# One block of 512 tokens in the last third of an input projection

## The chip, the cores and the metric

The kernel runs on one core of a Trainium2 chip. The metric is the device time of one execution in microseconds (us). The engines are TensorE (PE in the profile, its weight loads PEld), VectorE (DVE), ScalarE (ACT), GpSimd (POOL) and SyncE (SP), whose queue issues nearly all transfers.

## What is computed

One layer of a streaming encoder on 2064 tokens (16 learned meta tokens and 2048 of the sequence), 1024 features, all in float32. The part that matters here is the input projection, one product whose 2824 output columns are shared among three groups of heads:

```python
p = rms_norm(h, norm_mix_pre[l]) @ w_in[l]          # (2064, 1024) @ (1024, 2824)
pa, pb, pc = ...                                    # RG-LRU, forgetting attention (q, k, v, gate), RWKV-7
oa = rg_lru_group(xa, ya, ...)                      # a scan over tokens
ob = forgetting_attention_group(q, k, v, f_logit, f_bias)
oc = rwkv7_group(pc, ...)                           # a recurrence over tokens
h = h + rms_norm(concat([oa, ob, oc]) @ w_out[l], norm_mix_post[l])
f = causal_dwconv(rms_norm(h, norm_ffn_pre[l]) @ ffn_up[l], ffn_conv[l])
h = h + rms_norm((gelu(gate) * val) @ ffn_down[l], norm_ffn_post[l])
return h[:, 16:]
```

## The kernel before

Precision comes from splitting: every operand is held as a high and a low part in a reduced float32 format, and a product is three matmuls, high by high, high by low, low by high (`mm3`, L150 to L152).

The input projection goes over the tokens in three parts. Tokens come in 17 tiles, the first of 16 meta tokens and sixteen of 128. `w_in_tokens` (L158) cuts them into two blocks for each part: 400 and 384 tokens, 384 and 384, 256 and 256. `w_in_norm` (L165) loads each tile, scales it (L104 to L108), transposes it on TensorE (L121) and writes the high part with ScalarE (L127) and the low part with VectorE (L128) into the block's tiles `xh` and `xl`, which are allocated anew for each part under the tags `xh0`, `xl0`, `xh1`, `xl1` in a pool with one buffer for each tag.

`w_in_part` (L258) then runs over the output columns. First come the eight forget-gate columns (`w_in_gate`, L248 and L249), then 24 units of 128 columns: eight for RWKV, four for the LRU, four each for keys, values and queries. For a unit the weights are loaded and split (L143 to L145), and `w_in_step` (L186) does 24 matmuls for each block into one bank of PSUM (`psp`), then evacuates: for RWKV, LRU and values with either ScalarE or VectorE in turn (L55, L57), for queries and keys as a high part by ScalarE (L200, tile `sth`, two buffers) and a low part by VectorE (L201, tile `stl`, one buffer), each stored to scratch memory in DRAM (L202, L203). Values are turned by TensorE one step later (L217). The last two units run block by block, so that a block's tokens are done with before the other's:

```python
for block in blocks:
    for w, kind, c0 in last:
        step(w, block, kind, c0)
    yield
```

Beside the projection run the recurrences: `recurrences` (L1866) first handles the forget gate of each block (`gate_block`, L341), then LRU and RWKV blocks. They are advanced by `Beside`: at every `yield` of the projection 1.5 steps of the recurrences are emitted (`PACE`, L1827); what is left is emitted when the projection is over. The order of the program is not the order on the engines: the tile framework plans each engine's queue ahead (`TileContext(nc, schedule_with_timeline_sim=True)`, L2115), so that in the trace recurrence matmuls stand in the middle of a projection unit. On the chip each queue runs in its planned order.

After the third part the projection's pools are closed and attention (`Attn`) takes their memory; its constant rows are set by GpSimd (L435, L436, tile `k`) and VectorE (L431 to L433, tile `q`), and its loads are issued by SP (L470 to L499). A tile laid over old memory waits until the old tiles there have been read. Attention's scores are L635 and L636, its row maxima L509 to L515. Then follow the output projection (`pswo`) and the feed-forward layer (`psu`, `psd`).

Of the kernel before, what the change touches and what calls it, by code (L numbers as in the profile page):

```python
# [8 lines left out]
F32 = mybir.dt.float32  # L9
F32R = mybir.dt.float32r  # L10
# [8 lines left out]
P = 128  # L19
D = 1024  # L20
KD = D // P
# [126 lines left out]
def mm3(nc, out, ah, al, bh, bl, first, last, more=False):  # L148

    nc.tensor.matmul(out, ah, bh, start=first, stop=False, skip_group_check=more)  # L150
    nc.tensor.matmul(out, ah, bl, start=False, stop=False, skip_group_check=more)  # L151
    nc.tensor.matmul(out, al, bh, start=False, stop=last, skip_group_check=more)  # L152
# [5 lines left out]
def w_in_tokens(part):  # L158

    tiles = [(0, META)] + [(META + P * i, P) for i in range(SEQ // P)]  # L160
    cuts = ((0, 4, 7), (7, 10, 13), (13, 15, 17))[part]
    return [tiles[a:e] for a, e in zip(cuts, cuts[1:])]


def w_in_norm(core, pools, psum, x, meta, gain, part):  # L165
    blocks = []
    for b, tl in enumerate(w_in_tokens(part)):
        t0 = tl[0][0]
        n = sum(r for _, r in tl)
        hi = pools["xn"].tile([P, KD, n], F32R, tag=f"xh{b}", name=core.n("xh"))  # L170
        lo = pools["xn"].tile([P, KD, n], F32R, tag=f"xl{b}", name=core.n("xl"))
        blocks.append((t0, n, tl, hi, lo))
    for t0, n, tl, hi, lo in blocks:
        for s, rows in tl:
            src = meta if s < META else x[s - META : s - META + rows, :]
            norm_transpose(core, pools, psum, src, rows, gain, [(hi, lo, s - t0, 0, rows)])
    return blocks
# [8 lines left out]
def w_in_step(core, pools, psum, weights, block, kind, c0, scr):  # L186

    nc = core.nc
    wh, wl = weights
    st = pools["st"]  # L190
    t0, n, tl, hi, lo = block
    ps = psum.tile([P, 512], F32, tag="mm", name=core.n("psp"))
    for k in range(KD):
        mm3(nc, ps[:, :n], wh[:, k], wl[:, k], hi[:, k], lo[:, k], k == 0, k == KD - 1)
    if kind in ("q", "k"):
        sc = 0.125 if kind == "q" else 1.0
        r0 = c0 - (512 if kind == "q" else 1024)
        oh = st.tile([P, 400], F32R, tag="sth", name=core.n("sth"))
        ol = st.tile([P, 400], F32R, tag="stl", name=core.n("stl"), bufs=1)
        nc.scalar.activation(oh[:, :n], ps[:, :n], AF.Copy, scale=sc)  # L200
        nc.vector.scalar_tensor_tensor(ol[:, :n], ps[:, :n], sc, oh[:, :n], op0=ALU.mult, op1=ALU.subtract)  # L201
        nc.sync.dma_start(scr[kind + "h"][r0 : r0 + P, t0 : t0 + n], oh[:, :n].bitcast(F32))  # L202
        nc.sync.dma_start(scr[kind + "l"][r0 : r0 + P, t0 : t0 + n], ol[:, :n].bitcast(F32))  # L203
        return
    o = st.tile([P, 400], F32, tag="sth", name=core.n("stp"))
    core.evac(o[:, :n], ps[:, :n])
    if kind != "v":
        r0 = c0 if kind == "a" else c0 - 2056 + A_ROWS
        nc.sync.dma_start(scr["p"][r0 : r0 + P, PAD + t0 : PAD + t0 + n], o[:, :n])
        return  # L210

    def turn():

        r0 = c0 - 1536
        pt = psum.tile([P, 4, P], F32, tag="mm", name=core.n("psv"))
        for i, (s, rows) in enumerate(tl):
            nc.tensor.transpose(pt[:rows, i], o[:, s - t0 : s - t0 + rows], core.ident[:])  # L217
        ot = st.tile([P, 4, P], F32, tag="stv", name=core.n("stv"), bufs=1)
        i0 = 0
        if tl[0][1] < P:  # L220
            s, rows = tl[0]
            core.evac(ot[:rows, 0], pt[:rows, 0])
            nc.sync.dma_start(scr["v"][s : s + rows, r0 : r0 + P], ot[:rows, 0])
            i0 = 1
        m = len(tl)
        core.evac(ot[:, i0:m], pt[:, i0:m])
        s = tl[i0][0]
        nc.sync.dma_start(
            scr["v"][s : s + P * (m - i0), r0 : r0 + P].rearrange("(j p) c -> p j c", p=P), ot[:, i0:m]
        )  # L230

    return turn


def w_in_gate(core, pools, psum, w_in, blocks, scr):

    nc = core.nc
    c0 = 2048
    raw = pools["w"].tile([P, KD, 8], F32, tag="fraw", name=core.n("fraw"), bufs=1)
    nc.sync.dma_start(raw[:], w_in[:, c0 : c0 + 8].rearrange("(k p) c -> p k c", p=P))  # L240
    w = pools["w"].tile([P, KD, P], F32R, tag="wh", name=core.n("fw"))
    nc.vector.memset(w[:].bitcast(F32), 0.0)
    nc.scalar.activation(w[:, :, 0:8], raw[:], AF.Copy)
    nc.vector.tensor_tensor(w[:, :, 32:40], raw[:], w[:, :, 0:8], op=ALU.subtract)
    for t0, n, tl, hi, lo in blocks:
        ps = psum.tile([P, 512], F32, tag="mm", name=core.n("psf"))
        for k in range(KD):
            nc.tensor.matmul(ps[:, :n], w[:, k], hi[:, k], start=k == 0, stop=False)  # L248
            nc.tensor.matmul(ps[:, :n], w[:, k], lo[:, k], start=False, stop=k == KD - 1)  # L249
        a = pools["st"].tile([8, 400], F32, tag="sth", name=core.n("fa"))  # L250
        nc.scalar.activation(a[:, :n], ps[32:40, :n], AF.Copy)
        o = pools["st"].tile([8, 400], F32, tag="stl", name=core.n("fo"), bufs=1)
        nc.vector.tensor_tensor(o[:, :n], ps[0:8, :n], a[:, :n], op=ALU.add)
        nc.sync.dma_start(scr["f"][:, t0 : t0 + n], o[:, :n])
    yield
# [85 lines left out]
def gate_block(core, R, f_bias, scr, tl):  # L341

    nc = core.nc
    t0, n = tl[0][0], sum(r for _, r in tl)
    if t0 == 0:
        core.fb = core.const.tile([NH, 1], F32, name="fb")
        nc.sync.dma_start(core.fb[:], f_bias.rearrange("(h o) -> h o", o=1))

    def new(s, dt=F32):
        return R.t([NH, 400], s, dt)[:, :n]  # L350

    x = new("k")
    nc.sync.dma_start(x, scr["f"][:, t0 : t0 + n])
    a = new("r")
    nc.scalar.activation(a, x, AF.Abs, bias=core.fb[:])
    nc.scalar.activation(a, a, AF.Exp, scale=-1.0)
    nc.scalar.activation(a, a, AF.Ln, bias=1.0)
    nc.vector.tensor_scalar(x, x, core.fb[:], 0.0, op0=ALU.add, op1=ALU.min)
    nc.vector.tensor_tensor(x, x, a, op=ALU.subtract)

    o = META if t0 else 0
    call = R.t([NH, 512], "sq")[:, : o + n]
    c = call[:, o:]
    if o:
        nc.vector.tensor_copy(call[:, :o], core.ctail[:])
    nc.vector.tensor_tensor_scan(
        c, core.ones_8[:].to_broadcast([NH, n]), x, core.ctail[:, META - 1 :], op0=ALU.mult, op1=ALU.add
    )
    nc.vector.tensor_copy(core.ctail[:], c[:, n - META :])
    ch, cl = new("k", F32R), new("r", F32R)  # L370
    nc.scalar.activation(ch, c, AF.Copy, scale=-1.0)
    nc.vector.scalar_tensor_tensor(cl, c, -1.0, ch, op0=ALU.mult, op1=ALU.subtract)
    nc.sync.dma_start(scr["ch"][:, t0 : t0 + n], ch.bitcast(F32))
    nc.sync.dma_start(scr["cl"][:, t0 : t0 + n], cl.bitcast(F32))
    j0, full = (t0 - o) // P, (o + n) // P
    ps = R.pe()
    for i in range(full):
        nc.tensor.transpose(ps[:, NH * i : NH * i + NH], call[:, P * i : P * i + P], core.ident[:NH, :NH])
    js = slice(j0, j0 + full)
    nc.vector.tensor_copy(core.ccol[:, js].rearrange("p j h -> p (j h)"), ps[:, : NH * full])  # L380
    if t0 + n == T:
        ps = R.pe()
        nc.tensor.transpose(ps[:META, :NH], call[:, P * full :], core.ident[:NH, :NH])
        nc.vector.tensor_copy(core.ccol[:META, NKT - 1], ps[:META, :NH])
        js = slice(j0, j0 + full + 1)
    ps = R.pe()
    w = (js.stop - js.start) * NH
    nc.tensor.matmul(
        ps[:, :w], core.ones_row[:], core.ccol[0:1, js].rearrange("p j h -> p (j h)"), start=True, stop=True
    )  # L390
    nc.vector.tensor_copy(core.cref[:, js].rearrange("p j h -> p (j h)"), ps[:, :w])
# [1474 lines left out]
def recurrences(core, R, lk, f_bias, scr, blocks, part):  # L1866


    for blk in blocks:
        gate_block(core, R, f_bias, scr, blk[2])  # L1870
        yield
    for b in ((0, 1, 2), (3, 4, 5), (6, 7, 8))[part]:
        yield from lru_block(core, R, scr, lk, b)
        gen = R.block(b)
        while next(gen) != R.SOLVED:
            yield
        yield from R.ending
        R.ending = gen
# [240 lines left out]
```

## Time and profile before

| what | value |
|---|---|
| time, three runs | 3123.35, 3115.73 and 3134.21 us, median 3123.35 |
| profiled execution | 3122.89 us, of which the span of instructions is 3121.2 us |
| granted TensorE clock, mean | 0.962 |
| busy: PE, DVE, ACT, POOL | 2925.9, 2251.1, 1452.4, 1301.9 us |

The input projection fills the stretch from 44.7 to 869.3 us: part one to 290, part two to about 627, part three from 635 to 869. Attention lies between there and about 1600 us, with the rest of the recurrences beside it until about 1200 us; the feed-forward layer takes the rest.

A row of a group gives line, engine, operation, tile written and tiles read, shapes and number, then busy time, mean ns of one, and the idle time of its engine ahead of it with what ended it. A row of the order of time gives start, duration, engine and line, and in brackets the idle time ahead of it and what ended it. SPq is SP's queue issuing a transfer. A row of a window gives its bounds and length, busy time and number of instructions of PE, PEld, DVE, ACT and POOL, the granted clock, and the share and rate of the transfers. Ends of matmuls are modelled, and consecutive matmuls overlap in the records.

### The profile page before, as it was taken

To read this page: it belongs to the slowest core of one execution; us is meant where nothing else is said; L and a number is where in the kernel's file an instruction comes from. 1 tells how busy PE (TensorE), PEld (TensorE's weight loads), DVE (VectorE), ACT (ScalarE), POOL (GpSimd) and SP (SyncE) were. 2 spreads that over 40 slices of the span, in tenths; PEclk is the share of its full clock that TensorE was granted. 3 is DMA by queue.
4 is the path that set the end of the run, shared out by engine and by line. 5 is a ranking of instruction groups with operands and counts; after the bars stand their busy time and mean duration, and the time that the engine had idled before them with its cause. 6 is when DMAs were issued, how large, how long until landed. Compare 5 with 4: busy or idle time off the path is not lost. (4 is left out here: it accounts for less than half of the span.)

```text
span 3121.2 us, 52484 instructions
## 1 busy us (share of the span) xinstructions
PE 2925.9 (94%) x18488; PEld 2492.2 (80%) x18488; DVE 2251.1 (72%) x4585; ACT 1452.4 (47%) x2716; POOL 1301.9 (42%) x1436
## 2 busy tenths in 40 slices
PE   6988999999978999999998899999999999999998
PEld 6987998999855664665576899899999999787776
DVE  6247655676688778877758898888778787547777
ACT  4135334344544444445533555566666665324332
POOL 3310001101134365446733568743533334547665
PEclk9999999999988788999999899999999999999999
DMA  6664333353353235544236555565665565535454
GB/s 205 226 204 137 101 97 100 107 140 104 97 143 81 64 84 142 130 117 107 65 107 201 162 171 158 167 193 170 166 166 166 166 188 162 174 105 167 143 161 142
DMA packets 456503, 443.72 MB, mean 142 GB/s; under 512 B 82496, under 2 KB 373514, under 8 KB 453408
## 3 DMA queue, kind: packets, MB, share of 16 engines
q1 hardware_dynamic: 455856, 439.99, 48.3%
q8 instruction: 145, 2.38, 0.3%
q14 instruction: 118, 0.97, 0.1%
q0 software_dynamic: 384, 0.39, 0.0%
HBM read 314.39 MB, written 125.87 MB: 141 GB/s over the span
## 5 line engine op out<-in xcount | busy, mean ns | idle before, releaser
L150 PE MATMUL psu<-xo,uw 128*128 128x344 f32 x1848 | 594.9, 326 | 25.2 <-DVE vb L1684 10.4
L151 PE MATMUL psu<-xo,uw 128*128 128x344 f32 x1848 | 597.1, 323 | 0.7 <-DVE xo L1529 0.7
L152 PE MATMUL psu<-xo,uw 128*128 128x344 f32 x1848 | 586.5, 322 | 0.0
L150 PE MATMUL psp<-xh,wh 128*128 128x384 f32 (+2 forms) x1152 | 382.0, 332 | 0.0
L152 PE MATMUL psp<-xh,wl 128*128 128x384 f32 (+2 forms) x1152 | 379.1, 330 | 3.0 <-DVE wl L145 3.0
L151 PE MATMUL psp<-xl,wh 128*128 128x384 f32 (+2 forms) x1152 | 378.2, 328 | 0.0
L150 PEld LDWEIGHTS psu<-xo,uw 128*128 128x128 f32 x1848 | 350.3, 190 | 31.4 <-DVE vb L1684 12.4
L1529 DVE TENSOR_TENSOR uw<-uq,uw 128x512 fp32r<-128x512 f32 x352 | 327.5, 935 | 59.5 <-ACT uw L1528 55.8
L151 PEld LDWEIGHTS psu<-xo,uw 128*128 128x128 f32 x1848 | 351.7, 190 | 1.1 <-DVE xo L1529 1.1
L152 PEld LDWEIGHTS psu<-xo,uw 128*128 128x128 f32 x1848 | 350.0, 190 | 0.0
L1528 ACT ACTIVATE uw<-uq 128x512 fp32r<-128x512 f32 x462 | 286.9, 627 | 102.8 <-PE psu L152 48.8
L640 ACT ACTIVATE p<-sc,bias 128x512 f32<-128x512 f32 (+4 forms) x352 | 197.6, 590 | 217.3 <-PE sc L636 181.8
L1640 DVE SCALAR_TENSOR_TENSOR uy<-psu,ffn_cols,uy 128x342 f32<-128x342 f32 (+1 forms) x396 | 224.0, 567 | 72.0 <-ACT uy L1638 70.9
L679 POOL TENSOR_TENSOR acc<-acc,p 128x512 f32<-128x512 f32 (+3 forms) x208 | 230.5, 1111 | 78.7 <-DVE acc L679 37.9
L1646 POOL TENSOR_TENSOR uy<-uy,uy 128x342 f32<-128x342 f32 (+1 forms) x132 | 146.3, 1109 | 224.5 <-DVE uy L1640 79.2
L152 PEld LDWEIGHTS psp<-xh,wl 128*128 128x128 f32 x1152 | 220.1, 191 | 10.3 <-issue 5.5
L150 PEld LDWEIGHTS psp<-xh,wh 128*128 128x128 f32 x1152 | 219.9, 191 | 7.1 <-issue 4.7
L151 PEld LDWEIGHTS psp<-xl,wh 128*128 128x128 f32 x1152 | 220.0, 191 | 6.4 <-issue 4.1
L1529 POOL TENSOR_TENSOR uw<-uq,uw 128x512 fp32r<-128x512 f32 x110 | 155.9, 1417 | 164.2 <-ACT uw L1528 137.8
L512 DVE TENSOR_REDUCE mc<-mx 128x1 f32<-128x400 f32 (+5 forms) x320 | 171.5, 554 | 55.3 <-PE mx L509 53.9
L1529 DVE TENSOR_TENSOR fo<-u,fo 128x896 fp32r<-128x896 f32 x88 | 104.4, 1187 | 118.6 <-ACT fo L1528 118.6
L1528 ACT ACTIVATE fo<-u 128x896 fp32r<-128x896 f32 x88 | 81.0, 922 | 230.9 <-POOL u L1756 120.9
(451 smaller groups left out, 6612.6 us busy)
## 6 DMA issues: line engine op xcount, KB each, us to landing
uq<-in_ffn_up_dram SPq DMA_DIRECT2D x220, 256.0 KB
uq<-scr_us SPq DMA_DIRECT2D x176, 256.0 KB
raw<-in_w_in_dram SPq DMA_DIRECT2D x72, 512.0 KB
scr_us<-uq SPq DMA_DIRECT2D x88, 256.0 KB
u<-scr_ff SPq DMA_DIRECT2D x88, 256.0 KB
scr_ff<-uy SPq DMA_DIRECT2D x110, 171.0 KB
q<-scr_qh SPq DMA_DIRECT2D x96, 128.0 KB
ds<-in_ffn_down_dram SPq DMA_DIRECT2D x10, 1024.0 KB
```

Of the source, the lines that this page charges most:

```text
L150: nc.tensor.matmul(out, ah, bh, start=first, stop=False, skip_group_check=more)
L151: nc.tensor.matmul(out, ah, bl, start=False, stop=False, skip_group_check=more)
L152: nc.tensor.matmul(out, al, bh, start=False, stop=last, skip_group_check=more)
L512: self.reduced = nc.vector.tensor_reduce(mc[:rows, i, ci : ci + 1], ps[:rows, :full], axis=AX.X, op=ALU.max)
L640: last = nc.scalar.activation(p[:rows, :w], ps[:rows, :w], AF.Exp, bias=bias[:rows, j : j + 1])
L679: eng.tensor_tensor(a, ps_[0][0][:rows, c0:n] if start and i == 1 else a, p[:rows, : n - c0], op=ALU.add)
L1528: core.nc.scalar.activation(hi, src, AF.Copy)
L1529: (eng or core.nc.vector).tensor_tensor(lo, src, hi, op=ALU.subtract)
L1640: stt(y[:, :n], src[:, i : n + i], cw[:, 44 * i + cc : 44 * i + cc + 1], y[:, :n], op0=ALU.mult, op1=ALU.add)
L1646: core.pooled = nc.gpsimd.tensor_tensor(v[:, :n], g[:, :n], v[:, :n], op=ALU.mult)
```

## The change

The third part is cut into one block of 512 tokens. The high and low parts of the tokens live in two tiles of 784 columns, allocated once for all parts; the first block of a part lies at column 0, the second at column 400. The block of 512 of the third part therefore lies across what the two blocks of 384 of the second part used. Staging tiles grow from 400 to 512 columns. The forget gate of the block of 512 is still handled in two halves. As the last two units yield once for each block, the third part yields 24 times, not 25.

```diff
 def w_in_tokens(part):
 
     tiles = [(0, META)] + [(META + P * i, P) for i in range(SEQ // P)]
-    cuts = ((0, 4, 7), (7, 10, 13), (13, 15, 17))[part]
+    cuts = ((0, 4, 7), (7, 10, 13), (13, 17))[part]
     return [tiles[a:e] for a, e in zip(cuts, cuts[1:])]
+
+CUT, COLS, BANK = 400, 784, 512
 
 def w_in_norm(core, pools, psum, x, meta, gain, part):
     blocks = []
+    if part == 0:
+        core.tokens = [pools["xn"].tile([P, KD, COLS], F32R, tag=s, name=core.n(s)) for s in ("xh", "xl")]
     for b, tl in enumerate(w_in_tokens(part)):
         t0 = tl[0][0]
         n = sum(r for _, r in tl)
-        hi = pools["xn"].tile([P, KD, n], F32R, tag=f"xh{b}", name=core.n("xh"))
-        lo = pools["xn"].tile([P, KD, n], F32R, tag=f"xl{b}", name=core.n("xl"))
+        hi, lo = (t[:, :, CUT * b : CUT * b + n] for t in core.tokens)
         blocks.append((t0, n, tl, hi, lo))
...
-        oh = st.tile([P, 400], F32R, tag="sth", name=core.n("sth"))
-        ol = st.tile([P, 400], F32R, tag="stl", name=core.n("stl"), bufs=1)
+        oh = st.tile([P, BANK], F32R, tag="sth", name=core.n("sth"))
+        ol = st.tile([P, BANK], F32R, tag="stl", name=core.n("stl"), bufs=1)
...
-    o = st.tile([P, 400], F32, tag="sth", name=core.n("stp"))
+    o = st.tile([P, BANK], F32, tag="sth", name=core.n("stp"))
...
 def recurrences(core, R, lk, f_bias, scr, blocks, part):
 
-    for blk in blocks:
-        gate_block(core, R, f_bias, scr, blk[2])
-        yield
+    for _, n, tl, *_ in blocks:
+        for tiles in (tl,) if n <= CUT else (tl[: len(tl) // 2], tl[len(tl) // 2 :]):
+            gate_block(core, R, f_bias, scr, tiles)
+            yield
```

More of the change, by code (lines that the diff above doesn't have):

```diff
@@ L249, in w_in_gate @@
             nc.tensor.matmul(ps[:, :n], w[:, k], lo[:, k], start=False, stop=k == KD - 1)
-        a = pools["st"].tile([8, 400], F32, tag="sth", name=core.n("fa"))
+        a = pools["st"].tile([8, BANK], F32, tag="sth", name=core.n("fa"))
         nc.scalar.activation(a[:, :n], ps[32:40, :n], AF.Copy)
-        o = pools["st"].tile([8, 400], F32, tag="stl", name=core.n("fo"), bufs=1)
+        o = pools["st"].tile([8, BANK], F32, tag="stl", name=core.n("fo"), bufs=1)
         nc.vector.tensor_tensor(o[:, :n], ps[0:8, :n], a[:, :n], op=ALU.add)
```

## The prediction

> **What bounds the kernel now.** I read the page first, then busy time by windows around the part of the kernel that the change touches, then single rows in order of time.
>
> ```profile
> PE 2925.9 (94%) x18488; PEld 2492.2 (80%) x18488; DVE 2251.1 (72%) x4585; ACT 1452.4 (47%) x2716; POOL 1301.9 (42%) x1436
> PEclk9999999999988788999999899999999999999999
> ```
>
> TensorE is busy for 94% of the span, and its granted clock is near full but for slice 23 and slices 12 to 16 (78 us each, so 858 to 1248 us). The change acts on the third part of the input projection; its own stretch is found by the first gate matmul of that part (635.4 us) and the end of its last projection matmul (869.3 us).
>
> ```profile
> core 0: us, PE busy (x) PEld busy (x) DVE busy (x) ACT busy (x) POOL busy (x), PEclk, DMA share, GB/s
> 635.40:869.30 233.90, 231.70 (x2430) 210.13 (x2428) 160.49 (x370) 110.45 (x202) 21.98 (x41) 0.99 0.40 110
> 869.30:920.00 50.70, 32.30 (x286) 21.80 (x287) 45.42 (x130) 19.16 (x39) 15.33 (x21) 0.76 0.74 171
> 920.00:980.00 60.00, 49.92 (x423) 31.39 (x423) 54.87 (x164) 29.45 (x63) 27.31 (x47) 0.90 0.33 83
> 980.00:1100.00 120.00, 108.02 (x1008) 75.74 (x1006) 89.08 (x275) 50.15 (x115) 56.05 (x94) 0.76 0.27 69
> 1100.00:1200.00 100.00, 92.39 (x640) 57.41 (x638) 82.39 (x247) 38.77 (x82) 49.43 (x75) 0.84 0.39 91
> ```
>
> In the 233.9 us of the third part TensorE is busy for 231.7: it alone sets the pace there, and what shortens its queue shortens the stretch. Right behind it the picture turns: between 869.3 and 920 TensorE works 32.3 of 50.7 us and VectorE 45.4, and until 980 VectorE works 54.9 of 60. So time won on TensorE before 869 is kept only if VectorE is not handed work into the next 110 us in exchange.
>
> **The matmuls.** The third part runs 24 weight columns over its 512 tokens. Today each column takes 8 x 3 matmuls for each of two blocks of 256; the change makes it 8 x 3 of 512 columns.
>
> ```profile
> L150 PE MATMUL psp<-xh,wh 128*128 128x256 f32 x384 | 112.7, 294 | 0.0
> L151 PE MATMUL psp<-xl,wh 128*128 128x256 f32 x384 | 110.8, 289 | 0.0
> L152 PE MATMUL psp<-xh,wl 128*128 128x256 f32 x384 | 111.6, 291 | 0.0
> ```
>
> That is 1152 matmuls now and 576 afterwards; the gate adds 32 now, 16 afterwards. Their mean of 290 ns cannot be used as a price, since matmuls overlap: the price is the distance from start to start in an undisturbed stretch. Here are the first and last rows of three such stretches: 14 starts of 256 columns, 20 of 384, and 12 of 512 columns (output projection, the same triple of lines).
>
> ```profile
> 700.01 0.28 PE L151 MATMUL psp<-xl,wh 128*128 128x256 f32 x1
> ...
> 701.55 0.28 PE L152 MATMUL psp<-xh,wl 128*128 128x256 f32 x1
> 583.01 0.34 PE L150 MATMUL psp<-xh,wh 128*128 128x384 f32 x1
> ...
> 586.35 0.34 PE L151 MATMUL psp<-xl,wh 128*128 128x384 f32 x1
> 1601.69 0.40 PE L152 MATMUL pswo<-woh,ml 128*128 128x512 f32 x1
> ...
> 1604.22 0.39 PE L151 MATMUL pswo<-wol,mh 128*128 128x512 f32 x1
> ```
>
> 256 columns: 1.54 / 13 = 0.1185 us. 384: 3.34 / 19 = 0.1758. 512: 2.53 / 11 = 0.2300. Two of 256 cost 0.2369, one of 512 costs 0.2300: 0.0069 saved for each pair, and 592 pairs make 4.1 us. The straight line through 256 and 384 would put 512 at 0.2331, that is 3.8 ns a pair and 2.2 us; this is the low end. A gain of twice 4.1 us, for a clock that steps down under dense work less often, is the far end. I take 4.1, since the 512 row is a measurement of the very form that is added. Weight loads are halved too, but they ran beside matmuls already (the distance grows with the columns, 57 ns for 128 of them, and almost nothing is left at zero columns), so nothing more comes from them.
>
> The Trainium skill (TensorE: Matmul & The Clock Gate, Back-to-back issue gap) gives a fixed cost of about 2.5 ns for each matmul above its columns at 2.4 GHz; by that the pairs would save 592 x 2.5 ns = 1.5 us. The rows differ (118.5 ns where it has 109), and the sum goes by the rows. The same section also gives a sustained figure of 131 ns for 512 columns; the 230 ns here speak against that, and no weight is given to it.
>
> **The start of the third part.** The gate matmuls of the first block start today as soon as two of the four token tiles are split. With one block they need all four.
>
> ```profile
> 635.41 0.37 PE L248 MATMUL psf<-xh,fw 128*128 128x256 f32 x1
> 637.63 1.09 PE L1189 MATMUL rps<-rwsc,rwxu 64*64 64x128 f32 x16
> 638.65 1.20 PE L1201 MATMUL rps<-rww,rwsc 128*64 128x64 f32 x32
> 637.56 1.87 DVE L128 TENSOR_TENSOR xl<-pst,xh 128x512 fp32r<-128x512 f32 x3
> 306.24 1.22 PE L981 MATMUL eps<-rwwa,wa_up 64*128 64x256 f32 x2 [11.31 <-ACT rwe L982]
> ```
>
> VectorE finishes the low halves of the last tiles at 639.4 (three operations of about 0.62 us from 637.56). The first four of eight row groups of all tiles are there after the second, at 638.8, so the gate starts 3.4 us later than 635.41. Cover is the recurrence: the L1189 and L1201 groups (1.09 and 1.20 us) that ran in the middle of the gate can run ahead of it if their own inputs are there, which leaves 1.1 us. Bounds: 0 with full cover, and 11.3 us, which is what the border between parts one and two shows when a recurrence matmul that waits for ScalarE stands ahead of ready projection work in TensorE's queue. I take 2 us, near the 1.1 to 3.4. Everything before (parts one and two) keeps its instructions; the two fixed buffers can be overwritten region by region, and the two borders already write new tokens only after the old part's last matmuls, so that edit costs nothing there.
>
> **Paced steps.** The last two weight columns yield once for each block, so the third part yields 24 times instead of 25, and at PACE 1.5 that moves 1.5 recurrence steps from beside the projection to behind it. In TensorE time a step costs (233.9 - 1184 x 0.1185) / 37.5 = 2.5 us, so 3.7 us leave the stretch.
>
> ```profile
> L145 DVE TENSOR_TENSOR wl<-raw,wh 128x1024 fp32r<-128x1024 f32 x24 | 29.1, 1213 | 2.4 <-ACT wh L144 2.2
> L57 DVE COPY stp<-psp 128x256 f32<-128x256 f32 x19 | 8.0, 421 | 4.2 <-PE psp L152 4.1
> L201 DVE SCALAR_TENSOR_TENSOR stl<-psp,sth 128x256 fp32r<-128x256 f32 x15 | 6.8, 452 | 12.1 <-DMA scr_kl<-stl 8.9 <-DMA scr_ql<-stl 2.7 <-ACT sth L200 0.5
> ```
>
> Their VectorE share is (160.5 - 29.1 - 8.0 - 6.8) / 37.5 = 3.1 us a step: 4.7 us arrive in a stretch where VectorE is the busy one. Bounds -3.7 and +4.7; I take 0, because what TensorE loses VectorE gets. The skipped weight-sum step is run at the end of the same loop and stays covered.
>
> **Evacuations and stores.** One operation of 512 columns (L128 above, 0.62 us) takes the place of two of 0.42 to 0.45: some 0.2 us less for each, on an engine with 73 us idle in the stretch, so nothing on the path. The L201 row shows more: with one low buffer, VectorE stood 11.6 us waiting for the store of the previous block. Steps twice as long (24 x 0.23 = 5.5 us in place of 2.8) leave the store its time, so that wait should go; TensorE had no idle time from it, so I count 0, and it returns as a rival.
>
> **The end of the third part.**
>
> ```profile
> 863.44 1.84 POOL L435 MEMSET k<- 64x2080 f32 x1 [13.91 <-PE psp L152]
> 869.32 1.83 POOL L435 MEMSET k<- 64x2080 f32 x1 [4.04 <-PE psp L152]
> 871.24 3.62 POOL L436 MEMSET k<- 4x2080 f32 x2
> 868.98 0.28 PE L152 MATMUL psp<-xh,wl 128*128 128x256 f32 x1
> 871.82 0.42 DVE L201 SCALAR_TENSOR_TENSOR stl<-psp,sth 128x256 fp32r<-128x256 f32 x1 [0.67 <-DMA scr_ql<-stl]
> 872.27 0.32 SPq L203 DMA_DIRECT2D scr_ql<-stl  x1
> 874.84 0.40 SPq L472 DMA_DIRECT2D k<-scr_ch  x1
> 880.85 1.10 PE L635 MATMUL sc<-q,k 128*128 128x512 f32 x2 [1.88 <-DMA q<-scr_qh]
> ```
>
> The last store is issued 3.0 us after the last matmul, because its low part waits for the buffer. Without that wait it is one ScalarE and one VectorE pass, about 1.6 us: 1.4 us won. Against it, attention's first key memset could start at 863.44, when the first block was read for the last time; with one block both memsets come after the end, and the chain to 874.86 grows by 1.8 us, with the gate rows of the keys (L472) and the loads behind them on SP's queue. Bounds -1.4 and +1.8; I take +0.5, as the loads queue there in any case.
>
> **Sum:** -4.1 + 2 + 0 + 0 + 0.5 = -1.6 us on the profiled 3122.9 us (span 3121.2), which lies 0.5 us under the median of 3123.35. Forecast 3121 us, no change that can be told: a measurement of this kernel can tell about 0.5%, 15.6 us, from none. With all bounds together it runs from about 3110 to 3139.
>
> **Rivals.** *Slower: the border stalls.* With one block nothing of the projection is ready until the last tile is split, and if TensorE's queue has a waiting recurrence instruction first, as at 306.24, it loses 11.3 us, and the matmuls behind the gap run at a lower clock:
>
> ```profile
> 312.93 0.52 PE L249 MATMUL psf<-xl,fw 128*128 128x384 f32 x1
> 313.25 0.52 PE L248 MATMUL psf<-xh,fw 128*128 128x384 f32 x1
> ```
>
> 0.32 us apart instead of 0.176, for about ten of them, 1.5 us. In all +12.8 - 4.1 + 0.5: 3132 us. It decides once the wait passes 4 us. For it: the queue is in order, and this happened at the other border. Against: there the last two tiles were also loaded late, and the third part has only four tiles. The Trainium skill (TensorE: Matmul & The Clock Gate, HAM oscillation) puts the re-throttling at an idle gap of about 3.4 us; the trace agrees, the gap there was 11.3 us and the spacing behind it nearly doubled.
>
> *Faster: VectorE gets its 11.6 us back.* If recurrence work queued behind the waiting L201 then runs ahead, less of it is left after 869, where VectorE is the limit: -11.6 - 1.6, about 3110 us. Against: TensorE has no room before 869 for work brought forward.
>
> *Another order behind the projection.* The queues are drawn up as a whole, so a shift of a few us can order attention's opening otherwise. TensorE's idle time from 869.3 to 1200 adds up to 48 us (18.4 + 10.1 + 12.0 + 7.6); a third of it more or less, with the clock of 0.76 to 0.9 there, is 16 to 20 us either way: about 3103 or 3140.
>
> **Chances.** Forecast 0.50; stall 0.16; VectorE's gain 0.12; another order 0.22, with both signs alike. Beyond 15.6 us on the fast side lie most of the good order and a third of VectorE's case with some of the forecast's tail: 0.19. On the slow side the bad order, a third of the stall and a tail: 0.21. Same: 0.60. The range reaches to the two orders' prices, 3102 to 3142.
>
> **What would show it.** Right: 576 projection matmuls of 512 columns about 0.230 us apart; the L201 wait for its store gone; the third part 2 to 6 us shorter; both key memsets after the last projection matmul. Wrong: an idle gap of TensorE over 4 us near 636 us (stall); a stretch from the projection's end to 1200 us that differs by over 10 us from today's 331 (order); or a spacing of 512 columns other than 0.23.

## The result

| | before | after |
|---|---|---|
| time, median of 4 runs on one chip | 3122.85 us (3115.73 to 3134.21) | 3165.53 us (3158.40 to 3167.15) |
| profiled execution (span) | 3122.89 us (3121.2) | 3166.32 us (3164.6) |
| mean granted TensorE clock of that execution | 0.962 | 0.946 |

The changed kernel is slower: ratio 1.0121, 95% interval 1.0089 to 1.0154. That is a small change, but clear of the noise. The forecast was 3121 us, no change that can be told, and 3165.53 lies beyond the upper end of its range, 3142.

From the page of the changed kernel, the engines' busy time and the line of the granted clock:

```profile
PE 2949.4 (93%) x17896; PEld 2481.0 (78%) x17896; DVE 2248.9 (71%) x4566; ACT 1449.2 (46%) x2697; POOL 1299.4 (41%) x1436
PEclk9998999999877688999999999999999999999999
```

There are 592 matmuls fewer, as meant, and yet TensorE is busy for 23.5 us more. The digits of the clock show where: 8 8 7 8 8 has become 8 7 7 6 8 8, in slices 11 to 16 (79 us each, 791 to 1266 us), which is where the projection ends and attention begins. Busy time by windows, cut at the end of the projection and at attention's last matmul of `po`; the row of before first (its third part was quoted with the prediction), then the two of after:

```profile
869.30:1609.60 740.30, 668.86 (x4018) 416.34 (x4018) 574.63 (x1525) 341.04 (x655) 399.62 (x501) 0.91 0.41 102
```

```profile
631.90:823.80 191.90, 191.14 (x1326) 147.25 (x1326) 121.33 (x249) 79.30 (x128) 11.97 (x22) 1.00 0.44 124
823.80:1642.70 818.90, 731.26 (x4529) 468.62 (x4528) 609.57 (x1622) 367.60 (x706) 406.19 (x520) 0.86 0.38 94
```

The third part did not become 2 to 6 us shorter but 42: 233.9 to 191.9 us. The stretch behind it became 78.6 us longer, at a clock of 0.86 in place of 0.91. The four differences add up: -3.5 before the third part, -42.0 in it, +78.6 behind it and +10.3 from there to the end make 43.4 us, the difference of the spans. The last of them is small, and its cause is open: the code there is the same in both kernels, and the clock was 0.98 in both.

What moved can be read from the order in which TensorE's queue was planned, counted in matmuls of the recurrences (2313 in all, as planned; the trace shows most of them as two instructions, 4443, which write the tiles `rps` and `eps`):

```
                                                before   after
planned, third part's gate to its end              636     371
planned, behind the last projection matmul         860    1125
trace, third part's gate to its end               1227     718
trace, behind the last projection matmul          1666    2175
trace, projection matmuls in a row between
  two pieces of recurrence, third part, mean      16.0    14.0   (part two: 16.7)
```

The queue has a piece of recurrence after about 14 to 17 projection matmuls, whether these are 256, 384 or 512 columns wide. With half as many matmuls there are 41 such rows of them instead of 72, and 265 recurrence matmuls stand behind the projection that stood beside it before. That is not a fixed rule of the planner: in e4 below, with 192 and 128 columns, there are 29 and 24 matmuls between two pieces on the mean. What the planner weighs was not looked into. In the trace 509 recurrence instructions have moved; they make nearly all of the 512 that the third part's row has lost besides the 592 (2430 - 592 - 1326), and of the 511 that the row behind it has gained.

What such an instruction costs can be worked out on both sides. Beside the projection it is what the third part has left over when the projection's matmuls are taken out at their distances: (233.9 - 1184 x 0.1185) / 1227 = 0.076 us before, and (191.9 - 592 x 0.231) / 718 = 0.077 us after. Behind the projection the 509 that were added made the stretch 78.6 us longer, 0.154 us each. The rows of e5 below give 0.074 and 0.162 us in the same way. These are estimates, but they agree: the same work costs about twice as much there.

Granted clock in the stretch where they ended up, of after:

```profile
823.80:870.00 46.20, 37.87 (x427) 31.66 (x427) 35.70 (x109) 18.41 (x37) 19.09 (x32) 0.67 0.73 165
870.00:920.00 50.00, 37.82 (x215) 22.17 (x209) 41.04 (x123) 24.49 (x46) 17.70 (x23) 0.73 0.30 73
920.00:980.00 60.00, 54.59 (x462) 36.86 (x462) 48.90 (x131) 35.36 (x73) 23.27 (x44) 0.80 0.35 92
980.00:1100.00 120.00, 94.12 (x849) 69.36 (x848) 85.53 (x251) 41.88 (x99) 38.31 (x65) 0.70 0.21 52
1100.00:1200.00 100.00, 90.87 (x819) 60.82 (x818) 70.77 (x215) 37.99 (x80) 52.80 (x82) 0.79 0.28 70
```

Before, the last four windows had 0.76, 0.90, 0.76 and 0.84, and the first still lay in the projection, at 0.99. Each execution also carries its span and its mean granted clock. Their product is called its length at full clock here, and the rest of the span the part lost by the clock. This is a reckoning and not a measurement: a stretch in which TensorE waits for others would not be shorter at full clock. Over the four runs of after this product is 2991.6 us (mean span 3162.4, of which 170.8 went to the lower clock); the profiled execution of before has 3121.2 x 0.962 = 3002.6, with 118.6 lost. By this reckoning the change saved some 11 us and lost 52 us by the clock. Before is a single execution there; in the sessions below the kernel before loses 127 to 129 us on the mean, and against that the change loses some 42.

### The profile page after: what moved, and what is told of

Its sections match the earlier page's. It is cut to its first block, busy times and chain, and to the rows that moved or that the text cites. A ratio compares the mean times of both kernels' runs of the same rounds, so it can differ in the third digit from the quotient of the medians.

```text
span 3164.6 us, 51192 instructions
## 1 busy us (share of the span) xinstructions
PE 2949.4 (93%) x17896; PEld 2481.0 (78%) x17896; DVE 2248.9 (71%) x4566; ACT 1449.2 (46%) x2697; POOL 1299.4 (41%) x1436
## 5 line engine op out<-in xcount | busy, mean ns | idle before, releaser
L152 PE MATMUL psp<-xh,wl 128*128 128x384 f32 (+2 forms) x960 | 344.3, 359 | 3.0 <-DVE wl L145 3.0
L150 PE MATMUL psp<-xh,wh 128*128 128x384 f32 (+2 forms) x960 | 345.5, 360 | 0.2 <-ACT wh L144 0.2
L151 PE MATMUL psp<-xl,wh 128*128 128x384 f32 (+2 forms) x960 | 345.1, 359 | 0.0
L152 PEld LDWEIGHTS psp<-xh,wl 128*128 128x128 f32 x960 | 183.3, 191 | 17.0 <-issue 5.0
L150 PEld LDWEIGHTS psp<-xh,wh 128*128 128x128 f32 x960 | 182.7, 190 | 13.4 <-issue 3.5
L151 PEld LDWEIGHTS psp<-xl,wh 128*128 128x128 f32 x960 | 182.6, 190 | 12.4 <-issue 3.5
```

## The experiments

The theories are these. **A**: the recurrence work left behind is the whole loss; the wide matmuls matter only because the plan interleaves by number. **B**: the block of 512 itself costs something (its late start, longer steps, the border, the tiles). Later ones are named with their runs. All ratios are to the kernel before, run on the same chip in the same session; its medians there were 3131.8 to 3136.0 us.

**e1: the block of 512, issued as halves.** The changed kernel, but each projection matmul of the block goes as two of 256 columns.

```diff
-    for k in range(KD):
-        mm3(nc, ps[:, :n], wh[:, k], wl[:, k], hi[:, k], lo[:, k], k == 0, k == KD - 1)
+    for s in (slice(0, n // 2), slice(n // 2, n)) if n == BANK else (slice(0, n),):
+        for k in range(KD):
+            mm3(nc, ps[:, s], wh[:, k], wl[:, k], hi[:, k, s], lo[:, k, s], k == 0, k == KD - 1)
```

> The changed kernel, with each 512-column matmul of the third part issued as two of 256 columns into the same bank (first all 24 for the left half, then all 24 for the right). Tokens' buffers, the evacuations of 512 columns, stores, yields stay as changed. Theory A (queue order): the planned queue of TensorE puts about as many projection matmuls between two pieces of the recurrence whatever their width, so wide ones crowd the recurrence out; here 860 of the 2313 recurrence matmuls stand behind the last projection matmul, as in the kernel before, against 1125 in the changed one. A expects 3118 to 3128 us, third part about 232 us. Theory B (one block: its late start, its single bank, its long evacuations, the missing yield): about 3160 to 3168 us, third part near 196 us.

Measured: 3138.67 us, ratio 1.0023 (1.0004 to 1.0042), with 860 recurrence matmuls left behind, as before. Third part and stretch behind it:

```profile
631.10:868.60 237.50, 236.41 (x2454) 212.64 (x2452) 162.14 (x356) 110.03 (x186) 21.45 (x41) 0.99 0.40 112
868.60:1622.00 753.40, 682.34 (x4019) 424.65 (x4019) 570.88 (x1527) 342.76 (x655) 402.14 (x502) 0.90 0.41 100
```

The block, the buffers, the evacuations of 512 columns, the 24 yields and the split gate are all in this kernel; only the width of the matmul is not. About four fifths of the loss are gone with it. The time is 6.8 us above the kernel before of its session, somewhat more than A allowed (5 us), so B is left with something, at most 0.4%.

**e2: the fixed buffers alone.** The changed kernel, with the third part cut in two again.

```diff
-    cuts = ((0, 4, 7), (7, 10, 13), (13, 17))[part]
+    cuts = ((0, 4, 7), (7, 10, 13), (13, 15, 17))[part]
```

> The changed kernel with the third part cut into two blocks of 256 again; the two fixed token buffers and the staging tiles of 512 columns stay. Theory A: queue as before (860 left), 3120 to 3127 us. Theory C (the fixed buffers make a part wait for the whole of the one before): slower than before, 3130 to 3165 us, with idle time of TensorE at the two borders between parts.

Measured: 3133.89 us, ratio 1.0005 (0.9985 to 1.0026). The buffers cost nothing that can be told; theory C (a part waits for the whole of the one before) is left with 0.3% at most. The times expected were counted from the 3122.85 us of the first session, so it is the ratio that decides here and below.

**e3: the kernel before with two low staging buffers.** This takes away VectorE's wait for the store.

```diff
-        ol = st.tile([P, 400], F32R, tag="stl", name=core.n("stl"), bufs=1)
+        ol = st.tile([P, 400], F32R, tag="stl", name=core.n("stl"), bufs=2)
...
-        o = pools["st"].tile([8, 400], F32, tag="stl", name=core.n("fo"), bufs=1)
+        o = pools["st"].tile([8, 400], F32, tag="stl", name=core.n("fo"), bufs=2)
```

> The kernel before, with two buffers in place of one for the staging tile of the low parts, so that VectorE no longer waits for the store of the block before. Theory A: same queue share (860 left), 3118 to 3125 us. The prediction's faster rival (VectorE's 11.6 us come back): about 3110 us. Theory D (the store wait held the projection back in favour of the recurrence, and the change let it go): toward 3140 to 3165 us, more than 860 left behind.

Measured: 3124.80 us, ratio 0.9984 (0.9968 to 1.0000). What L201 waited for in the third part, from the groups of that line (before it was 8.9 us for `scr_kl` and 3.4 for `scr_ql`):

```profile
L201 DVE SCALAR_TENSOR_TENSOR stl<-psp,sth x16: 401/420/968, 752.7 to 863.0; 128x256 fp32r<-128x256 f32 x16
  ACT sth L200: 2.6, 3
```

The wait is gone, and it is worth 0 to 10 us, 5 as the middle. That is the best of all the versions run, but not one that is clearly faster than before. Theory D, which expected 3140 us and more, falls.

**e4: the kernel before, all three parts issued as halves.** If narrow matmuls cost nothing extra, more interleaving should help.

```diff
-    for k in range(KD):
-        mm3(nc, ps[:, :n], wh[:, k], wl[:, k], hi[:, k], lo[:, k], k == 0, k == KD - 1)
+    for s in (slice(0, n // 2), slice(n // 2, n)):
+        for k in range(KD):
+            mm3(nc, ps[:, s], wh[:, k], wl[:, k], hi[:, k, s], lo[:, k, s], k == 0, k == KD - 1)
```

> The kernel before, with every projection matmul of all parts issued as two of half the columns (200, 192 and 128). Theory A: the recurrence gets more room; 630 of its matmuls stand behind the projection instead of 860. The change left 265 more and cost 42 us, so 230 fewer give about -37 us; 3456 more matmuls at some 4 ns each cost 14 us; in all near 3100 us. Theories B to D see only the added matmuls: 3137 us or more.

Measured: 3584.56 us, ratio 1.1442 (1.1374 to 1.1510): a plain miss. The first and last of a dense row of 200 columns at full clock (12 starts), of one of 128 columns at full clock (25 starts), of one of 128 columns at a lowered clock (21 starts), and the line of the granted clock:

```profile
60.20 0.28 PE L150 MATMUL psp<-xh,wh 128*128 128x200 f32 x1
...
61.43 0.27 PE L152 MATMUL psp<-xh,wl 128*128 128x200 f32 x1
```

```profile
772.25 0.27 PE L150 MATMUL psp<-xh,wh 128*128 128x128 f32 x1
...
774.93 0.27 PE L150 MATMUL psp<-xh,wh 128*128 128x128 f32 x1
```

```profile
899.70 0.41 PE L152 MATMUL psp<-xh,wl 128*128 128x128 f32 x1
...
903.97 0.41 PE L151 MATMUL psp<-xl,wh 128*128 128x128 f32 x1
```

```profile
PEclk9999899985555556898999999999999999999999
```

200 columns cost 1.23 / 11 = 0.112 us, scarcely less than 256 (0.1185). 128 columns cost the same, 2.68 / 24 = 0.112, and 4.27 / 20 = 0.213 where the clock is 0.5. So there is a least price of 0.112 us for such a matmul at full clock, and nearly twice that at half the clock. Halving 256 columns won nothing for each half, and the projection ended at 1370 us instead of 869. Busy time by windows at the end of the projection and behind it:

```profile
900.00:1370.40 470.40, 470.40 (x2716) 442.66 (x2715) 131.36 (x294) 89.45 (x160) 18.16 (x39) 0.52 0.14 39
1370.40:2087.20 716.80, 642.98 (x3580) 392.13 (x3579) 536.07 (x1447) 330.42 (x633) 383.16 (x483) 0.90 0.43 102
```

With 630 recurrence matmuls left behind instead of 860, the stretch behind took 716.8 us instead of 740.3: the side of A, at a price that no one would pay.

**e5: the kernel before, with recurrence left behind.** The matmuls stay 256 wide, and only the rate at which recurrence steps are emitted in the third part is lowered, so that 1139 matmuls are left behind.

```diff
+                if part == 2:
+                    beside.pace = 0.6
```

> The kernel before, two blocks of 256, with the pace of the recurrence lowered from 1.5 to 0.6 steps at each yield of the third part. 1139 of 2313 recurrence matmuls then stand behind the last projection matmul (1125 in the changed kernel, 860 in the kernel before). Theory A (what costs is the recurrence left for the stretch beside attention): 1139 - 860 = 279 more at 42/265 us each, +44 us, about 3167 to 3175 us, with the projection over near 825 us and a granted clock of about 0.75 up to 1250 us. Theory B (the block of 512 itself costs): 3123 to 3132 us.

Measured: 3171.96 us, ratio 1.0123 (1.0093 to 1.0154), the change's loss without any of the change's edits. Third part and the stretch behind it:

```profile
635.40:826.60 191.20, 190.75 (x1894) 179.62 (x1893) 112.06 (x238) 77.76 (x140) 12.99 (x23) 1.00 0.46 125
826.60:1654.10 827.50, 730.69 (x4557) 468.59 (x4556) 626.46 (x1656) 374.96 (x716) 410.83 (x519) 0.87 0.38 93
```

These are the rows of the changed kernel over again: 191.2 against 191.9 us, then 827.5 against 818.9 at 0.87 and 0.86.

**e6 and e7: the changed kernel, with the projection held back.** A unit's matmuls in the third part may run only behind the last recurrence matmul that was emitted 10 steps earlier (e6) or 3 steps earlier (e7). That leaves 826 and 736 recurrence matmuls behind, fewer than before the change. The rival, E, is that the recurrence is a chain with latencies of its own, so that TensorE will wait for it.

```diff
-    for k in range(KD):
-        mm3(...)
+    with core.tc.issue_after(core.hold) if core.hold is not None else nullcontext():
+        for k in range(KD):
+            mm3(...)
...
+                    core.hold = beside.behind(10) if part in (2,) else None   # e7: 3
```

> The changed kernel, with the matmuls of each unit of the third part queued behind the recurrence matmul that was emitted ten steps earlier; 826 left behind the projection. Theory A: 34 fewer than before at 0.16 us, and 4 us from the wider matmuls: 3110 to 3122 us. Theory B: above 3155 us. Theory E (the recurrence's own latency sets its pace, so holding the projection leaves TensorE idle): idle time of TensorE over 10 us in the third part, 3135 us or more.

> As the run with ten steps, with three: 736 left. Theory A: 124 fewer than before, -20 - 4 us, about 3100 us. Theory E: the gaps grow, 20 us and more of idle time in the third part, and the total is no better than with ten steps.

Measured: 3175.99 us, ratio 1.0136 (1.0100 to 1.0173), and 3181.72 us, ratio 1.0160 (1.0123 to 1.0197). Third part and the stretch behind it, e6 and then e7:

```profile
635.00:915.00 280.00, 253.91 (x1891) 193.69 (x1892) 175.44 (x394) 112.31 (x192) 20.69 (x43) 0.90 0.35 96
915.00:1661.80 746.80, 672.61 (x3964) 421.47 (x3962) 545.12 (x1478) 334.41 (x643) 393.31 (x499) 0.89 0.41 99
```

```profile
635.00:935.20 300.20, 265.56 (x2066) 200.53 (x2065) 182.87 (x415) 116.28 (x199) 28.03 (x56) 0.87 0.32 90
935.20:1662.60 727.40, 653.53 (x3791) 404.37 (x3790) 544.38 (x1461) 333.79 (x638) 388.10 (x486) 0.91 0.42 101
```

The work left behind is as small as wanted, and the stretch behind is back near 740 us or below. But now TensorE stands idle for 26 and 35 us in a third part of 280 and 300 us, at a clock of 0.90 and 0.87. E is right, and A must be put more narrowly: recurrence work left behind costs, and so does waiting for it. What the kernel seems to need is dense work enough to lie beside the recurrence's latencies. The third part of before had that, 234 us of it at 0.99.

**e8: half the dose.** The changed kernel, but 12 of the 24 units go as halves.

```diff
+    for s in (slice(0, n // 2), slice(n // 2, n)) if n == BANK and kind in ("c", "a") else (slice(0, n),):
```

> Dose. As the changed kernel, but 12 of the 24 units of the third part (those of RWKV and the LRU that come first) go as two halves of 256 columns, the other 12 stay 512 wide; 971 recurrence matmuls stand behind the last projection matmul in TensorE's queue (before 860, changed 1125). If the loss follows the recurrence work left behind (A): (971 - 860) / 265 x 42.7 us = 18 us over the kernel before, ratio 1.0057 (between 1.002 and 1.009), third part about 213 us long, the stretch from its end to attention's end about 775 to 785 us. If a single wide stretch is enough to bring the loss, whatever its length (B): near 1.012. If it is the tail of the third part alone that counts, where wide units still stand (C): also near 1.012, with the stretch behind near 819 us.

Measured: 3149.38 us, ratio 1.0052 (1.0034 to 1.0070), where A had said 1.0057 and the others about 1.012.

```profile
632.00:845.30 213.30, 212.19 (x1912) 180.14 (x1909) 136.57 (x299) 92.75 (x152) 20.42 (x37) 0.99 0.42 117
845.30:1627.70 782.40, 710.12 (x4241) 443.62 (x4240) 592.54 (x1578) 356.74 (x686) 402.83 (x505) 0.88 0.40 98
```

A's two lengths, about 213 and 775 to 785 us, came out as well. Ordered by recurrence matmuls left behind beyond those of before, the kernels in which nothing waits for the recurrence give:

```
left behind   ratio
    0         1.0005 (e2), 1.0023 (e1), 0.9984 (e3)
 +111         1.0052 (e8)
 +265         1.0121 (the change)
 +279         1.0123 (e5)
```

That is 0.44 to 0.47% for each hundred. Left out are e4, e6 and e7, whose projection costs more or waits, and e9, where attention moved too.

**e9: dense matmuls put between.** The changed kernel, with 73 extra matmuls of constants, 128x128 by 128x512, each into a tile of PSUM that the recurrence then overwrites. Does filling TensorE's gaps bring the clock back?

```diff
         ps = self.psum.tile([P, 512], F32, tag="at", name=self.core.n("rps"), bufs=2)
+        if self.warm:
+            w, x = self.warm
+            self.nc.tensor.matmul(ps[:], w[:], x[:], start=True, stop=True)
```

> As the changed kernel, with 73 extra matmuls (128x128 by 128x512, constants) on TensorE behind the projection, each ahead of a group of recurrence matmuls whose first write overwrites it: 73 x 0.23 us = 16.8 us of extra work, between about 824 and 1250 us. If the lowered clock there comes from TensorE's gaps and the price is paid through it, the granted clock of 870 to 1200 us rises from 0.70 to 0.80 to 0.85 or more and the time stays or falls: -20 to +5 us against the changed kernel, ratio to the kernel before 1.006 to 1.014. If the clock does not depend on such fill, it stays at 0.70 to 0.80 and the extra work at that clock costs +17 to +24 us where TensorE is the bound: ratio 1.018 to 1.020. If the fill falls into gaps and the clock stays, ratio 1.012 to 1.014 with the clock unchanged.

Measured: 3310.20 us, ratio 1.0559 (1.0503 to 1.0615), outside all three expectations. The plan answered with another order: the recurrence ran alone after the projection, and attention's first score came at 1143 us instead of 844. Windows of the stretch alone, of attention behind it, and of a part of the first; then the group of the added matmuls, with busy time and mean:

```profile
825.30:1143.30 318.00, 259.17 (x2249) 191.73 (x2248) 167.95 (x488) 85.35 (x179) 41.70 (x80) 0.56 0.10 25
1143.30:1789.10 645.80, 574.30 (x2353) 327.00 (x2353) 438.38 (x1135) 288.13 (x527) 358.34 (x440) 0.92 0.44 107
980.00:1100.00 120.00, 110.64 (x1022) 82.78 (x1021) 47.22 (x154) 22.61 (x55) 23.65 (x42) 0.56 0.04 8
```

```profile
L942 PE MATMUL rps<-warm,warm 128*128 128x512 f32 x73 | 56.2, 773 | 6.6 <-DVE rww L1263 3.7 <-ACT rww L1283 2.1 <-ACT rwxu L1283 0.5
```

Their records last 773 ns on the mean, about twice the 0.39 us that such a record has at full clock (the changed kernel at 820.78 us, below). At the stretch's clock the 73 x 0.23 = 16.8 us come to about 30 us, an estimate, so the filling was dearer than expected. The run does not answer its question, since attention was moved as well. It shows that the recurrence by itself, filled up with 73 wide matmuls, runs at 0.56, and that the gaps which the record shows do not explain that: from 980 to 1100 us TensorE is busy for 110.6 of 120 us, against 94.1 in the changed kernel, where the clock was 0.70.

## Why the prediction was wrong

**The step that failed is "Paced steps".** It counted what the program emits (24 yields, 1.5 steps fewer) and took that for what runs beside the projection. The queue is planned after emission: not 1.5 steps of 2.5 us left the third part but 265 matmuls, and with them some 38 of its 42 us. They came back behind the projection as 78.6 us. The term was 0 us, with bounds of -3.7 and +4.7; e5, which moves 279 matmuls and leaves the block as it was, prices it at 1.0123, some 38 us, and e8 shows that it grows about in proportion. The warning was there to be counted in the order of TensorE's queue before the change: between two pieces of recurrence stand as many projection matmuls at 256 columns (16.0 in the trace) as at 384 (16.7).

**The price behind the projection was sized by the wrong thing.** Idle time of TensorE was weighed there, 48 us, and VectorE as the limit. What grew, by the reckoning of span and clock, was the loss by the clock. Means over all runs of each kernel, each beside the kernel before of its session:

```
                        span     at full clock   lost by the clock
before (7 runs)         3132.6       3004.2            128.5
e5, left behind (4)     3170.2       3005.3            164.9
e6, held back 10 (4)    3174.3       3003.7            170.6
before (13 runs)        3130.7       3001.9            128.9
e8, half dose (10)      3147.2       3003.6            143.5
```

Within a session these differ at full clock by 2 us at most, and the lost part makes the difference; single executions of one kernel scatter by 8 us and more to either side there. For e6 the agreement hides something: it has the wide matmuls of the changed kernel, which comes to 2991.6 us (in the first session), so some 12 us of its waiting are there at full clock too. In e5 and e8 the lost part goes with the amount of recurrence that does not run beside dense projection. Whether it is caused by what those matmuls are (64 or 32 rows and columns), by how they are spaced or by the mix with attention, no run separates; e9, which was to, moved attention instead. e7 is an exception: of its 48 us, 20 are there at full clock too (3024.4), and 28 by the clock.

**The matmuls were right.** Rows of after in order of time:

```profile
820.78 0.39 PE L152 MATMUL psp<-xh,wl 128*128 128x512 f32 x1
...
823.55 0.39 PE L152 MATMUL psp<-xh,wl 128*128 128x512 f32 x1
```

12 distances in 2.77 us, 0.2308 us each, against 0.230 predicted. By these distances the pairs save 592 x 0.0061 = 3.6 us, against 4.1 predicted. The 11 us at full clock given above hold it, and what the rest of them is stays open, as single executions of before scatter by about as much.

**The start was priced too high, and the border does not stall.**

```profile
628.88 0.70 PE L986 MATMUL eps<-rwwa,wa_up 64*128 64x256 f32 x2
629.50 1.53 PE L121 MATMUL pst<-ident,xt 128*128 128x128 f32 x12
631.89 0.50 PE L253 MATMUL psf<-xh,fw 128*128 128x512 f32 x1 [0.86 <-DVE rwr L1382]
632.23 0.40 PE L150 MATMUL psp<-xh,wh 128*128 128x512 f32 x1
```

TensorE is idle for 0.86 us, where 2 were counted and the rival needed over 4. The rival of the stall (3132 us) fell.

**VectorE's wait went, and brought nothing back.** Line L206 (L201 of before) in the third part of after:

```profile
L206 DVE SCALAR_TENSOR_TENSOR stl<-psp,sth x8: 672/684/1999, 738.5 to 825.7; 128x512 fp32r<-128x512 f32 x8
  ACT sth L205: 1.7, 1
```

The waits for stores are gone, as foreseen. e3 takes the same waits from the kernel before and measures 0 to 10 us; the rival at 3110 us, 13 below, is not borne out, though a smaller gain of its kind is possible.

**The end was priced too low.**

```profile
824.07 3.60 POOL L440 MEMSET k<- 64x2080 f32 x2 [7.48 <-PE psp L152]
824.29 3.40 DVE L370 COPY rwsq<-ctail 8x16 f32<-8x16 f32 x1
825.70 2.00 DVE L206 SCALAR_TENSOR_TENSOR stl<-psp,sth 128x512 fp32r<-128x512 f32 x1
827.77 0.34 SPq L208 DMA_DIRECT2D scr_ql<-stl  x1
830.96 0.39 SPq L477 DMA_DIRECT2D k<-scr_ch  x1
```

Both memsets come after the last projection matmul, as predicted. But beside them VectorE's last operation took 2.00 us instead of 0.68, and the last store was issued 3.8 us after the last matmul's end, where the kernel before had 3.0 and 1.6 was foreseen. The gate rows of the keys (L477) follow the start of that matmul by 7.4 us, before by 5.9: +1.5 instead of +0.5.

By these rows VectorE's operation (L206) was not slow by itself: a copy of 8x16 numbers stood ahead of it in VectorE's queue (L370) and took 3.40 us, where the other four of its line took about 0.15. That copy ended at 827.69 us, and the memsets at 827.67. The Trainium skill (SBUF — State Buffer, SBUF: two separate sides) describes a pair of ports shared by VectorE and GpSimd: an operation of VectorE in a two-port mode and one of GpSimd lock each other out, and whichever starts first holds the pair for the whole instruction. The two ends agree with that; the trace does not show in which mode the copy ran, and no run tested it. It is a small part of the loss, and e1, which keeps this edit, bounds it.

**"Another order behind the projection" was the right kind of case.** Its sign to watch, a stretch from the projection's end to 1200 us more than 10 us off 331, shows 376. But that sign was badly chosen: its end is fixed, so it grows by every us by which the projection ends earlier, and that is all of its growth. The stretch that tells is the one to attention's end, 740.3 us before and 818.9 after. The rival was also thought of as chance, alike in both signs, and at 16 to 20 us. It was neither: the order followed from making the matmuls half as many and twice as wide, since e1 undoes that alone and has the old order back. It had one sign, and the kernel lost 43 us.

The Trainium skill (TensorE: Matmul & The Clock Gate, Part 1: The HAM clock gate) holds that sustained matmul activity releases the throttle, and idleness brings it back. The runs agree for the projection at 256 columns and more (0.99 and 1.00 in the third part), and do not agree for e4's: 470.4 us of narrow matmuls without a gap in the record, at 0.52. Here the measurement decides, with one reserve: ends of matmuls are modelled, so that gaps shorter than a matmul cannot be seen. What kind of work leaves the clock low stays open.

## What to carry to other kernels

Where a planner interleaves two streams, a change in the number of instructions of one stream can move the other: count in the planned queue what stands on which side of a border, before costing anything by what the program emits. A phase of dense matmuls is worth more than its own work, since a chain of small dependent matmuls runs beside it at full clock, here at about half the price; a shorter dense phase can be the slower kernel. Multiply span by granted clock for each kernel that is compared: it is a quick first split into work and clock, and no more than that, as it does not see who waits for whom.

## What was not expected of the hardware

The projection's matmuls have a least price: 0.112 us at 128 and at 200 columns, against 0.1185 at 256, all at full clock (e4 and the kernel before); at a clock of 0.5 it is 0.213 at 128 columns. The prediction read the fixed cost as almost nothing from 256 and 384 columns, and there it is; below 256 it isn't.

The granted clock can stay low while TensorE's record is full: 0.52 over 470 us with 470 busy (e4), 0.56 with 110.6 of 120 busy (e9).
